# Softmax denominators in a two-layer DiT block: one 0/1 product and a wide reciprocal in place of a turn, a narrow reciprocal and a spread

## The chip, the cores and the metric

The kernel runs on one core of a Trainium2 chip. The metric is device microseconds for one execution. Engines are named as in the profile: PE is TensorE (PEld its weight loads), DVE is VectorE, ACT is ScalarE, POOL is GpSimd, SP is SyncE, whose queue issues the DMA transfers. All engines run their own instruction streams in order and wait for each other through semaphores.

## The reference, cut to what matters

The reference is a block of depth two over 512 tokens (and 256 context tokens) of width 1024, float32 throughout. Layer 0 is a Fourier/Hyena mixer, layer 1 is multi-head latent attention with 16 heads; a gated convolutional feed-forward part follows each. The change lies in the attention of layer 1:

```python
s = jnp.einsum('bqhd,bkhd->bhqk', qblk, k, preferred_element_type=jnp.float32) * scale
p = jax.nn.softmax(s, axis=-1).astype(v.dtype)
return jnp.einsum('bhqk,bkhv->bqhv', p, v)
```

For each of 16 heads there are 512 queries and 512 + 256 = 768 keys, 96 features for a score and 64 for a value. The kernel doesn't normalize the probabilities: it multiplies the values with exp(s - max) and divides the product, 64 rows by 512 queries, by the sum of the exponentials of each query. Only how these sums are brought together, inverted and brought to the rows of the product is changed.

## The kernel before, in words

Tokens lie along the free dimension and features on partitions. A float32 product that needs full precision is made of three single-pass products of high and low parts (`mm3`, lines 123 to 125) where both operands are split; other products are plain float32 (the profile shows two records, one weight load and one product each, per plain float32 product).

`attention` (line 949) first makes the latents, the values `V` and the normalized query latents. Then it goes over eight pairs of heads, p = 0 to 7. Three helpers make a pair:

- `qk(p)` (1081 to 1132): query and key projections of the pair (products into tiles `s` and `k2`), squares of them on ACT, their sums through small products into `ms` (lines 1100, 1112, 1114), a reciprocal square root on DVE (lines 1116 to 1120 and 132 to 141, some fourteen tiny instructions in a row), key parts `Kh` and `Kl` (ACT and DVE), and eight products with the identity that spread the roots over the tile (line 1130), with which DVE scales the queries (line 1131).
- `scores(p, a)` (1134 to 1156) for head a of the pair: six score tiles of 128 keys by 512 queries (three products each), copied to SBUF by ACT with the key's scale (line 1145) into two tiles `S` of three; maxima on DVE (lines 1146 to 1149), over the partitions on POOL (line 1151), and then, for each of the two tiles, the subtraction on DVE (line 1154, 128 x 1536) and the exponential on ACT (line 1155).
- `attend(p)` (1158 to 1186): 12 products with ones (line 1164), each 32 columns wide, which leave four partial sums of the denominators in four quarters of the PSUM tile `z`, two quarters a head; then the chain that is changed; 12 products with the values (line 1176), each 64 columns wide, two of which run side by side, into `pv`; and the product of `pv` with the row of inverted denominators into `O[p]` (line 1186).

The chain that is changed, before: ACT copies `z` to `zc` (1167). Four products turn it, 128 queries at a time, with a 128 x 2 matrix of zeros and ones as the moving operand, so that queries lie on partitions and the two columns are the sums of the two heads (1170). DVE inverts these 128 x 8 numbers (1172). Eight products with the identity spread them back over 64 partitions a head (1182). ACT copies that to `zrow` (1185), and line 1186 uses it. Each of `z`, `zt`, `zb` in the code is one tile of the same single PSUM buffer `z`, as `pv` is a single buffer, so the first product into each waits for the last reader of the one before.

The driving loop (lines 1188 to 1198) prepares two pairs ahead: in iteration p it emits `scores(p)`, `qk(p + 2)` and `attend(p - 1)`. The order in which the instructions stand on each engine is not this order but is made by the tile framework's scheduler when the kernel is built, with its own estimates; at run time every engine keeps to it. In what it made, PE has, ahead of the scores of pair p + 1, the eight spreading products of line 1130 of `qk(p + 2)`, which wait for the reciprocal square root on DVE. `attend(p - 1)` and `attend(p)` both fall into the same iteration for p = 1, 3 and 5, and none of them is finished in the iterations between, so that the iterations alternate in length. In this text iteration p runs from the first score product of pair p to the first of pair p + 1; those of p = 1, 3 and 5 are called long and those of p = 2 and 4 short. After the last pair the outputs `O` are split into high and low parts (`oh`, `ol`, lines 1209 and 1210), and the output projection `w_o` and the second feed-forward part follow.

Of the kernel before, what the change touches and what calls it, by code (L numbers as in the profile page):

```python
# [9 lines left out]
F32 = mybir.dt.float32  # L10
# [8 lines left out]
P = 128  # L19
# [31 lines left out]
class Builder:  # L51
# [897 lines left out]
    def attention(self, x, hh, hl, rest):  # L949
        nc, I = self.nc, self.I  # L950
        v = nc.vector
# [15 lines left out]
        ssp = self.t(pa, [P, 20], F32, "ssp")  # L967
        ones1 = self.ones32[:, 0:1]
        msk = self.t(pa, [P, 266], F32, "msk")
        rot, zsel, qm, ksel, s4 = msk[0:64, 0:128], msk[:, 128:130], msk[:, 256:258], msk[:, 258:260], msk[:, 260:264]  # L970
        qm32 = self.t(pa, [P, 2, 32], F32, "qm32")

        pt = self.pool("pt", bufs=2)
# [101 lines left out]
        pq = self.pool("pq", bufs=2)  # L1075
# [82 lines left out]
        def attend(p, Ss):  # L1158
            pv = self.t(psB, [P, 512], F32, "pv", 1)
            Z = lambda: self.t(psB, [P, 512], F32, "z", 1)  # L1160
            z = Z()
            for k in range(3):
                for g in range(4):
                    nc.tensor.matmul(z[32 * g : 32 * g + 32, :], self.ones32, Ss[g // 2][(2 * k + g % 2) // 3][:, (2 * k + g % 2) % 3, :], start=k == 0, stop=k == 2,  # L1164
                                     tile_position=(0, 32 * g))
            zc = self.t(pq, [P, 512], F32, "zc", 1)
            nc.scalar.copy(zc, z)
            zt = Z()
            for t_ in range(4):
                nc.tensor.matmul(zt[:, 2 * t_ : 2 * t_ + 2], zc[:, P * t_ : P * t_ + P], zsel, start=True, stop=True)  # L1170
            rz = self.t(pq, [P, 8], F32, "rz", 2)
            v.reciprocal(rz, zt[:, 0:8])
            for k in range(6):
                for a in range(2):
                    h = 2 * p + a
                    nc.tensor.matmul(pv[64 * a : 64 * a + 64, :], V[:, k, 64 * h : 64 * h + 64], Ss[a][k // 3][:, k % 3, :], start=k == 0, stop=k == 5,  # L1176
                                     tile_position=(0, 64 * a))
            zb = Z()
            for t_ in range(4):
                for a in range(2):  # L1180
                    g = 2 * t_ + a
                    nc.tensor.matmul(zb[64 * a : 64 * a + 64, P * t_ : P * t_ + P], rz[:, g : g + 1].to_broadcast([P, 64]), self.ident,
                                     start=True, stop=True, tile_position=(0, 64 * a))
            row = self.t(pq, [P, 512], F32, "zrow", 1)
            nc.scalar.copy(row, zb)
            v.tensor_tensor(O[p], pv, row, op=ALU.mult)

        prep = {0: qk(0), 1: qk(1)}
# [1 line left out]
        for p in range(KD):  # L1190
            qs, rs = prep.pop(p)
            Ss = [scores(p, a, qs[a], rs) for a in range(2)]
            if p + 2 < KD:
                prep[p + 2] = qk(p + 2)
            if prev:
                attend(*prev)
            prev = (p, Ss)
        attend(*prev)
        self.dbg("O", O)
        self.close("Sp")  # L1200
# [55 lines left out]
def constants():  # L1256
# [70 lines left out]
    am = np.zeros((P, 266))  # L1327
    j = np.arange(128)
    am[:64, 0:128] = (np.arange(64)[:, None] % 32) == (j[None, :] % 32)
    am[0::32, 128:130] = (np.arange(4)[:, None] // 2) == np.arange(2)[None, :]  # L1330
    am[:, 256] = np.arange(P) < 96
    am[:, 257] = (np.arange(P) < 32) | (np.arange(P) >= 64)
    am[:64, 258] = 1.0
# [86 lines left out]
def arrays_of(inputs):  # L1420
    a = layouts(**{k: np.asarray(v) for k, v in inputs.items()})
    a.update(constants())
    return {k: np.ascontiguousarray(v) for k, v in a.items()}
# [16 lines left out]
```

## Time and profile before

| What | us |
|---|---|
| Median of 3 runs (lowest, highest) | 1831.08 (1829.17, 1833.47) |
| Profiled execution | 1830.64 |
| Its span in the trace | 1828.8 |
| PE busy in the span | 1706.3 |
| DVE busy | 1022.0 |
| ACT busy | 613.9 |

In the profile "L1176" is line 1176 of the kernel before. A row of a group has the line, the engine, the operation, the tiles (out<-in), the shapes, the number of instructions, the total and the mean time, and the idle time of the engine ahead of them with what ended it. A row of the timeline has the start and the duration in us. A plain float32 product counts two matmul records. The two products of line 1170 and line 1182 write tiles that the profile names `z`, as the sums of line 1164 do.

### The profile page before, as it was taken

To read this page: it belongs to the slowest core of one execution; us is meant where nothing else is said; L and a number is where in the kernel's file an instruction comes from. 1 tells how busy PE (TensorE), PEld (TensorE's weight loads), DVE (VectorE), ACT (ScalarE), POOL (GpSimd) and SP (SyncE) were. 2 spreads that over 40 slices of the span, in tenths; PEclk is the share of its full clock that TensorE was granted. 3 is DMA by queue.
4 is the path that set the end of the run, shared out by engine and by line. 5 is a ranking of instruction groups with operands and counts; after the bars stand their busy time and mean duration, and the time that the engine had idled before them with its cause. 6 is when DMAs were issued, how large, how long until landed. Compare 5 with 4: busy or idle time off the path is not lost.

```text
span 1828.8 us, 21719 instructions
## 1 busy us (share of the span) xinstructions
PE 1706.3 (93%) x8742; PEld 1326.3 (73%) x8742; DVE 1022.0 (56%) x1662; ACT 613.9 (34%) x830; POOL 121.3 (7%) x202
## 2 busy tenths in 40 slices
PE   6889975799899999999999887899998999999999
PEld 2657864787688888888888556555554777888887
DVE  3486966864898435543434554665764554444443
ACT  3332222323323212222122434655663443223231
POOL 0052113310000000000000000110110000000000
PEclk7799987899999999999999998899999999999999
DMA  9032520352355234431312310000002323322322
GB/s 351 24 127 71 171 78 30 103 173 81 116 174 176 88 104 140 147 128 70 121 47 85 117 60 24 1 12 12 12 12 70 116 72 101 104 93 92 104 75 98
DMA packets 53249, 172.83 MB, mean 95 GB/s; under 512 B 6043, under 2 KB 8925, under 8 KB 52125
## 3 DMA queue, kind: packets, MB, share of 16 engines
q1 hardware_dynamic: 53149, 171.45, 27.4%
q8 instruction: 69, 1.13, 0.2%
q14 instruction: 31, 0.25, 0.0%
HBM read 167.23 MB, written 4.19 MB: 94 GB/s over the span
## 4 chain that ended last, share of the span: by engine, by line
PE 77%; DVE 11%; ACT 5%; POOL 3%; issue 3%; DMA 1%; POOLq 0%; SPq 0%; ACTq 0%; DVEq 0%
PE mm L123 21%; PE mm L124 20%; PE mm L125 20%; PE pv L1176 2%; PE ms L234 2%; PE z L1164 2%; DVE junk L210 2%; DVE wl L103 1%; DVE S L1154 1%; PE s L1130 1%; ACT S L1145 1%; PE s L123 1%; PE s L124 1%; PE s L125 1%; POOL s L388 1%
## 5 line engine op out<-in xcount | busy, mean ns | idle before, releaser
L123 PE MATMUL mm<-hh,wh 128*128 128x512 f32 (+2 forms) x1344 | 474.7, 356 | 7.0 <-ACT wh L98 3.4
L124 PE MATMUL mm<-hl,wh 128*128 128x512 f32 (+2 forms) x1344 | 473.9, 353 | 4.9 <-DVE hl L271 4.6
L125 PE MATMUL mm<-hh,wl 128*128 128x512 f32 (+2 forms) x1344 | 473.2, 353 | 1.3 <-DVE wl L103 1.3
L98 ACT ACTIVATE wh<-wr 128x1024 fp32r<-128x1024 f32 (+2 forms) x200 | 206.2, 1031 | 717.5 <-PE mm L124 646.5
L103 DVE TENSOR_TENSOR wl<-wr,wh 128x1024 fp32r<-128x1024 f32 (+2 forms) x200 | 243.6, 1219 | 287.3 <-ACT wh L98 279.6
L123 PEld LDWEIGHTS mm<-hh,wh 128*128 128x128 f32 x1344 | 254.4, 190 | 57.1 <-issue 12.0
L124 PEld LDWEIGHTS mm<-hl,wh 128*128 128x128 f32 x1344 | 255.0, 190 | 42.9 <-DVE hl L271 7.5
L125 PEld LDWEIGHTS mm<-hh,wl 128*128 128x128 f32 x1344 | 254.5, 190 | 38.4 <-issue 2.5
L123 PE MATMUL mm<-ah,wh 128*128 128x512 f32 (+1 forms) x528 | 187.8, 356 | 0.0
L124 PE MATMUL mm<-al,wh 128*128 128x512 f32 (+1 forms) x528 | 187.7, 356 | 0.0
L125 PE MATMUL mm<-ah,wl 128*128 128x512 f32 (+1 forms) x528 | 187.3, 355 | 0.0
L210 DVE SCALAR_TENSOR_TENSOR junk<-wr,sb 128x1024 bf16<-128x1024 f32 x128 | 159.3, 1244 | 36.7 <-DMA wr<-wmodT 36.6
L808 DVE SCALAR_TENSOR_TENSOR xr<-mm,mod,xr 128x512 f32<-128x512 f32 (+1 forms) x100 | 62.2, 642 | 204.3 <-PE mm L125 204.0
L123 PEld LDWEIGHTS mm<-ah,wh 128*128 128x128 f32 x528 | 99.1, 188 | 19.2 <-DVE xr L808 2.5
L124 PEld LDWEIGHTS mm<-al,wh 128*128 128x128 f32 x528 | 99.2, 188 | 15.3 <-issue 0.8
L125 PEld LDWEIGHTS mm<-ah,wl 128*128 128x128 f32 x528 | 99.2, 188 | 14.6
L1145 ACT ACTIVATE S<-s,rks 128x512 f32<-128x512 f32 x96 | 63.4, 688 | 44.3 <-PE s L125 43.4
L1154 DVE TENSOR_TENSOR S<-S,mb 128x1536 f32<-128x1536 f32 x32 | 54.8, 1752 | 20.7 <-POOL mb L1151 20.7
L845 ACT ACTIVATE fg<-fg 128x772 f32<-128x772 f32 (+1 forms) x44 | 32.6, 741 | 100.3 <-DVE fg L324 89.3
L1176 PE MATMUL pv<-S,V 128*64 128x512 f32 x192 | 58.9, 620 | 0.0
L1164 PE MATMUL z<-S,ones 128*32 128x512 f32 x192 | 42.7, 699 | 13.7 <-ACT S L1155 11.3
L1155 ACT ACTIVATE S<-S 128x1536 f32<-128x1536 f32 x32 | 47.1, 1481 | 18.0 <-DVE S L1154 18.0
(318 smaller groups left out, 2282.6 us busy)
## 6 DMA issues: line engine op xcount, KB each, us to landing
wr<-w_up SPq DMA_DIRECT2D x88, 512.0 KB, 3.3
wr<-wmodT SPq DMA_DIRECT2D x80, 512.0 KB, 3.3
wr<-w_dn SPq DMA_DIRECT2D x32, 512.0 KB, 3.2
wm<-wmod0a SPq DMA_DIRECT2D x8, 1024.0 KB, 9.6
wr<-w_in SPq DMA_DIRECT2D x16, 512.0 KB, 3.2
wr<-w_dn SPq DMA_DIRECT2D x20, 384.0 KB, 3.1
wr<-w_out SPq DMA_DIRECT2D x12, 512.0 KB, 3.2
wr<-w_o SPq DMA_DIRECT2D x12, 512.0 KB, 3.2
```

The costliest lines, as they stand in the source:

```text
L98: self.nc.scalar.activation(dst, src, AF.Copy)
L103: (eng or self.nc.vector).tensor_tensor(dst, src, hi.bitcast(F32), op=ALU.subtract)
L123: mmul(out, wh, xh, start=start, stop=False)
L124: mmul(out, wh, xl, start=False, stop=False)
L125: mmul(out, wl, xh, start=False, stop=stop)
L210: nc.vector.scalar_tensor_tensor(junk, raw, 1.0, self.sb[:, j, :], op0=ALU.mult, op1=ALU.mult, accum_out=acc)
L808: nc.vector.scalar_tensor_tensor(x[m][:, a2:b2], ps[:, a2:b2], mod[:, 8 * sec + m, j : j + 1], x[m][:, a2:b2], op0=ALU.mult, op1=ALU.add)
L1145: nc.scalar.activation(S[j // 3][:, j % 3, :], ps, AF.Copy, scale=rs[:, 2 * j + a : 2 * j + a + 1])
L1154: v.tensor_tensor(s, s, mb3.to_broadcast([P, 3, T]), op=ALU.subtract)
L1155: nc.scalar.activation(s, s, AF.Exp)
L1164: nc.tensor.matmul(z[32 * g : 32 * g + 32, :], self.ones32, Ss[g // 2][(2 * k + g % 2) // 3][:, (2 * k + g % 2) % 3, :], start=k == 0, sto ...
L1176: nc.tensor.matmul(pv[64 * a : 64 * a + 64, :], V[:, k, 64 * h : 64 * h + 64], Ss[a][k // 3][:, k % 3, :], start=k == 0, stop=k == 5, tile ...
```

## The change

The turning products, the narrow reciprocal, the spreading products and ACT's copy go. In their place, one product has a 128 x 128 matrix of zeros and ones (`zsum`) as the stationary operand and `zc` as the moving one: each of its 128 output rows is the sum of the two quarters of its head, so the denominators of all 512 queries stand on all 64 rows of each head at once. DVE then takes the reciprocal of the whole 128 x 512 tile out of PSUM into `zrow`. `msk` keeps its size; the matrix takes columns that were empty.

```diff
-        rot, zsel, qm, ksel, s4 = msk[0:64, 0:128], msk[:, 128:130], msk[:, 256:258], ...
+        rot, zsum, qm, ksel, s4 = msk[0:64, 0:128], msk[:, 128:256], msk[:, 256:258], ...
...
             zt = Z()
-            for t_ in range(4):
-                nc.tensor.matmul(zt[:, 2 * t_ : 2 * t_ + 2], zc[:, P * t_ : P * t_ + P], zsel, start=True, stop=True)
-            rz = self.t(pq, [P, 8], F32, "rz", 2)
-            v.reciprocal(rz, zt[:, 0:8])
+            nc.tensor.matmul(zt, zsum, zc, start=True, stop=True)
+            row = self.t(pq, [P, 512], F32, "zrow", 1)
+            v.reciprocal(row, zt)
             for k in range(6):
...
-            zb = Z()
-            for t_ in range(4):
-                for a in range(2):
-                    g = 2 * t_ + a
-                    nc.tensor.matmul(zb[64 * a : 64 * a + 64, P * t_ : P * t_ + P], rz[:, g : g + 1].to_broadcast([P, 64]), self.ident,
-                                     start=True, stop=True, tile_position=(0, 64 * a))
-            row = self.t(pq, [P, 512], F32, "zrow", 1)
-            nc.scalar.copy(row, zb)
             v.tensor_tensor(O[p], pv, row, op=ALU.mult)
...
-    am[0::32, 128:130] = (np.arange(4)[:, None] // 2) == np.arange(2)[None, :]
+    am[0::32, 128:256] = (np.arange(4)[:, None] // 2) == (j[None, :] // 64)
```

The scheduler makes a new order from the changed program. What it moves on PE and DVE, in iteration p = 3 (lines in the numbering of the kernel before; products are counted, not records):

```
DVE before: ... subtract x2 | reciprocal 128x8 | ql | max 1146 | qt | max 1147, 1148, 1149 | wl | subtract x2 | qt |
            nrm_s | Kl | 1117 | O2 | 132 | Kl | 133 | reciprocal 128x8 | 9 tiny | 1120 | 1131 x2
DVE after:  ... subtract x2 | reciprocal 128x512 | max 1146 | qt | max 1147, 1148 | qt | max 1149 | O2 | subtract x2 |
            nrm_s | Kl | 1117 | ql | 132 | wl | 133 | Kl | 4 tiny | reciprocal 128x512 | 2 tiny | O3 | 3 tiny | 1120 | 1131 x2
PE before:  ... 10 of line 1164 | 1 of 1176 | 4 of 1170 | 2 of 1176 | 6 of k2 | 2 of 1176 | line 1130 | scores
PE after:   ... 1 of 1176 | 5 of 1164 | 2 of 1176 | 5 of 1164 | 2 of 1176 | 1 of 1170 | 6 of k2 | 7 of 1176 | line 1130 | scores
```

In p = 5 the order is of the same kind, without the six k2 products and with O5 ahead of the seven tiny instructions; in p = 1 the ten sums of line 1164 stay together, ten products of line 1176 stand ahead of line 1130, and no O stands between the second reciprocal and the tiny instructions. In both kernels the last pairs have their own order; there the changed kernel has the reciprocal of pair 6 and O6 between the maxima 1146 and 1149 of the last head.

More of the change, by code (lines that the diff above doesn't have):

```diff
@@ L969, in attention @@
         msk = self.t(pa, [P, 266], F32, "msk")
-        rot, zsel, qm, ksel, s4 = msk[0:64, 0:128], msk[:, 128:130], msk[:, 256:258], msk[:, 258:260], msk[:, 260:264]
+        rot, zsum, qm, ksel, s4 = msk[0:64, 0:128], msk[:, 128:256], msk[:, 256:258], msk[:, 258:260], msk[:, 260:264]
         qm32 = self.t(pa, [P, 2, 32], F32, "qm32")
```

## The prediction

> **What bounds the kernel now.** I read the page first, then the timeline and the stretches around the attention of layer 1.
>
> ```profile
> span 1828.8 us, 21719 instructions
> ...
> PE 1706.3 (93%) x8742; PEld 1326.3 (73%) x8742; DVE 1022.0 (56%) x1662; ACT 613.9 (34%) x830; POOL 121.3 (7%) x202
> ...
> PE 77%; DVE 11%; ACT 5%; POOL 3%; issue 3%; DMA 1%; POOLq 0%; SPq 0%; ACTq 0%; DVEq 0%
> ```
>
> PE is busy and carries most of the chain, DVE comes second. All that changes lies between 1130 and 1400 us. By stretches (limits, length, busy time with counts of PE, PEld, DVE, ACT, POOL, then the granted clock):
>
> ```profile
> 1130.00:1400.00 270.00, 248.92 (x1249) 141.91 (x1250) 171.20 (x271) 155.67 (x206) 28.55 (x16) 0.94 0.05 18
> ...
> 1236.00:1297.00 61.00, 60.21 (x319) 35.55 (x317) 37.98 (x62) 35.90 (x50) 7.13 (x4) 0.99 0.03 10
> ...
> 1301.00:1305.00 4.00, 3.83 (x17) 1.78 (x14) 3.63 (x16) 1.83 (x2) 0.00 (x0) 0.57 0.00 0
> ```
>
> No engine is full there: DVE works 171 of 270 us. What counts is order and waiting. The first score products of pairs 1 to 6 (PE timeline) cut it into iterations:
>
> ```profile
> 1171.34 0.48 PE L123 MATMUL s<-qh,Kh 128*128 128x512 f32 x1
> ...
> 1207.95 0.47 PE L123 MATMUL s<-qh,Kh 128*128 128x512 f32 x1
> ...
> 1239.35 0.48 PE L123 MATMUL s<-qh,Kh 128*128 128x512 f32 x1
> ...
> 1275.77 0.48 PE L123 MATMUL s<-qh,Kh 128*128 128x512 f32 x1
> ...
> 1307.01 0.48 PE L123 MATMUL s<-qh,Kh 128*128 128x512 f32 x1
> ...
> 1342.89 0.47 PE L123 MATMUL s<-qh,Kh 128*128 128x512 f32 x1
> ```
>
> Long ones take 36.6, 36.4 and 35.9 us, short ones 31.4 and 31.2. Both divisions fall into the long ones. The long iteration of pair 3, by the timeline:
>
> ```profile
> 1249.65 3.43 DVE L1154 TENSOR_TENSOR S<-S,mb 128x1536 f32<-128x1536 f32 x2 [1.98 <-POOL mb L1151]
> ...
> 1251.77 2.79 PE L1176 MATMUL pv<-S,V 128*64 128x512 f32 x12
> ...
> 1255.57 1.23 DVE L1146 TENSOR_TENSOR mx<-S,S 128x1024 f32<-128x1024 f32 x1 [1.82 <-ACT S L1145]
> ...
> 1257.44 0.68 DVE L1147 TENSOR_TENSOR mx<-mx,S 128x512 f32<-128x512 f32 x1
> 1258.04 0.68 DVE L1148 TENSOR_TENSOR mx<-mx,S 128x512 f32<-128x512 f32 x1
> 1258.76 0.69 DVE L1149 TENSOR_TENSOR mx<-mx 128x512 f32<-128x512 f32 x1
> ...
> 1260.36 1.04 PE L1182 MATMUL z<-cst,rz 128*64 128x128 f32 x12
> ...
> 1261.67 3.42 DVE L1154 TENSOR_TENSOR S<-S,mb 128x1536 f32<-128x1536 f32 x2
> ...
> 1263.67 2.93 ACT L1155 ACTIVATE S<-S 128x1536 f32<-128x1536 f32 x2
> ...
> 1265.99 2.77 PE L1164 MATMUL z<-S,ones 128*32 128x512 f32 x20
> ...
> 1269.70 1.05 PE L1170 MATMUL z<-msk,zc 128*128 128x2 f32 x8
> ...
> 1270.79 0.21 DVE L1172 RECIPROCAL rz<-z 128x8 f32<-128x8 f32 x1 [1.60 <-PE z L1170]
> ...
> 1272.57 0.18 DVE L141 SCALAR_TENSOR_TENSOR rq_r<-rq_b,rq_r 128x20 f32<-128x20 f32 x1
> ...
> 1273.96 2.05 PE L1130 MATMUL s<-cst,rq_r 128*128 128x128 f32 x16
> ```
>
> The reader is to see one rope: subtraction for head 0, maxima, POOL, subtraction and exponential for head 1, its sums, the small reciprocal, the nine tiny root instructions queued behind it on DVE, line 1130, the next scores. PE's own work just covers it at the end: the root is ready at 1272.75, PE gets to line 1130 at 1273.96.
>
> **The change part by part.** Prices, from groups by shape (from the stretch 1130 to 1400, and of the whole run for line 412, which has the very shape, PSUM source included, of the added reciprocal) and one row of the timeline for the nearest full-width float32 product:
>
> ```profile
> L1182 PE MATMUL z<-cst,rz 128*64 128x128 f32 x128 | 13.8, 278 | 0.0
> ...
> L1170 PE MATMUL z<-msk,zc 128*128 128x2 f32 x64 | 8.4, 254 | 0.0
> ...
> L1185 ACT COPY zrow<-z 128x512 f32<-128x512 f32 x8 | 4.7, 584 | 15.5 <-PE z L1182 15.5
> ...
> L1172 DVE RECIPROCAL rz<-z 128x8 f32<-128x8 f32 x8 | 1.6, 205 | 14.3 <-PE z L1170 14.3
> ...
> L412 DVE RECIPROCAL S<-ms 128x512 f32<-128x512 f32 x2 | 6.7, 3346 | 0.0
> ...
> 103.48 1.13 PE L410 MATMUL ms<-s,on 128*128 128x512 f32 x2 [0.70 <-POOL s L394]
> ```
>
> - Turn (1170): 1.05 us a pair goes, a full product comes. Line 410 bounds it by 1.13 from above; four side-by-side value products of two records (2.79 for 12 records, six products in three turns) give 0.93 from below. I take 0.95: nothing gained or lost.
> - Spread (1182): 13.8 us of summed durations, but pieces overlap; twelve of a pair's sixteen records take 1.04 in the long iteration and the other four run beside the last value product: some 1.2. Between 0 and 13.8 / 8 = 1.7. Off PE it frees at most 8 x 1.2 = 9.8 us, where PE is the end of the rope.
> - Copy (1185): 0.58 us less of ACT a pair, seldom at the end of anything.
> - Reciprocal: 3.35 - 0.21 = 3.14 us more of DVE a pair, 25.1 in all. DVE has the room (171 + 25 of 270), but not at these places.
> - SP and POOL keep their instructions; transfers (5% share here) are not what is late.
>
> [...]
>
> Long iteration, pair 3, followed in the changed order. Head 0's subtraction ends at 1253.08. The first wide reciprocal comes next, to 1256.43 (its product is done long before). The maximum 1146 had waited for ACT till 1255.57, so only 0.86 is lost here; with one more `qt` ahead of 1149 (0.6, as from 1147 to 1148, from start to start) 1149 ends at about 1260.75 instead of 1259.45. POOL takes the usual 1.98, head 1's subtraction starts at 1262.7 instead of 1261.67, its exponentials end at 1267.75 (+1.15). PE has no spread to do and waits for them. The sums are now cut: five after the first exponential (from 1266.1; ten took 2.77 in three turns of up to four, five take two turns, 1.85), two value products (1.0), five sums (1.85), two value products (1.0): 1271.8, the new product to 1272.7, where the turn ended at 1270.75. The second reciprocal runs to 1276.1. Behind it on DVE stands O3, which needs all value products. PE does k2 first (from the turn's start to line 1130 passed 4.26, less 1.05 and two turns of value products leaves 1.3), then seven value products in four turns of 0.93: 1277.7. O3 0.6, three tiny ones (nine took 1270.95 to 1272.75, 0.2 each) and line 1130 starts at 1279.05: **+5.1**. Pair 5: no k2, seven tiny instructions after O5: 1272.7 + 3.72 + 0.6 + 1.5 = 1278.6, **+5.2** against its own start. Pair 1: sums uncut, the product ends at 1271.5, ten value products in five turns and k2 end at 1277.4, and the root is ready by 1276.4: **+3.3**. Together +13.6. From below: with the product where the turn ended, the reciprocal and 1.5 us of tiny work still make line 1130 start at 1275.7, +1.7 each, 5 in all.
>
> Short iterations (pair 4), by DVE's timeline and PE's:
>
> ```profile
> 1292.96 0.68 DVE L1149 TENSOR_TENSOR mx<-mx 128x512 f32<-128x512 f32 x1
> ...
> 1295.88 0.18 DVE L1116 TENSOR_TENSOR nrm_s<-ms,ssp 128x20 f32<-128x20 f32 x1 [2.24 <-PE ms L1114]
> ...
> 1296.85 3.41 DVE L1154 TENSOR_TENSOR S<-S,mb 128x1536 f32<-128x1536 f32 x2
> ...
> 1305.20 2.05 PE L1130 MATMUL s<-cst,rq_r 128*128 128x128 f32 x16
> ```
>
> Here something is won. DVE waited 2.24 for key sums that stood behind value products and the spread on PE; those are gone, so the subtraction follows POOL at 1293.64 + 1.98 = 1295.62: 1.2 earlier. In pair 4, O (0.6) leaves the stretch too: -1.9. In pair 2 it stays, and PE's sums and k2 products after the exponentials hold the gain to some -0.9. From above: 0 each.
>
> The end, where nothing else covers:
>
> ```profile
> 1381.06 3.43 DVE L1154 TENSOR_TENSOR S<-S,mb 128x1536 f32<-128x1536 f32 x2 [1.35 <-POOL mb L1151]
> ...
> 1384.45 3.62 PE L1164 MATMUL z<-S,ones 128*32 128x512 f32 x10 [3.36 <-ACT S L1155]
> ...
> 1392.93 1.05 PE L1170 MATMUL z<-msk,zc 128*128 128x2 f32 x8
> ...
> 1399.15 0.69 DVE L1186 TENSOR_TENSOR O<-pv,zrow 128x512 f32<-128x512 f32 x1 [4.91 <-ACT zrow L1185]
> ```
>
> The reciprocal of pair 6 and O6 stand among the last head's maxima (+3.14 and +0.6, less 0.6 for O5 and about 1 of a wait for ACT): +2.0 on the last subtraction. Then product at 1394.9 to 1395.9, reciprocal to 1399.25, the last value products to 1399.6; O7 at 1399.65 instead of 1399.15, since spread and copy are gone: **+0.5** net.
>
> Sum: 13.6 - 0.9 - 1.9 + 0.5 = +11.3 on 1830.64, its own execution: 1841.9. That execution lies 0.44 under the median of the runs shown, so I say 1842.
>
> **The rivals.** First, DVE's slack hides every reciprocal and PE's saving counts. It needs the rope to end on PE: that PE, not the root, is what line 1130 waits for, by more than the 3.14 that DVE gains. The stretch shows 1.2 us of such room (1272.75 to 1273.96), and PE's 98.7% busy between the scores of pair 3 and the first wait speaks for it. Then the 9.8 of above go: 1821. It decides the sign if the second reciprocal starts before about 1269, before its sums are done in the old order.
>
> Second, every reciprocal lies on the rope in full and no short iteration gives back: 8 x 3.14 = 25, less the spread and copy at the very end (1.8): 1854. Against it: head 0's reciprocal falls partly into DVE's 1.82 us of waiting for ACT.
>
> Third, the clock. The stretch 1301 to 1305 shows 0.57 of the granted clock after PE had waited; such a stretch costs 4 x 0.43 = 1.7 us. Long iterations show none now. If the longer waits put one into each, 3 x 1.7 = 5.2 come on top: 1847. [...]
>
> Fourth, gains and losses cancel, as with +1.7 for each long iteration, 3.1 won in the short ones and 1.8, the spread and the copy, at the end, the last head's maxima being covered: 1831. For it speaks that the floor is a floor, against it that head 1's exponentials are late by more than a microsecond in each long iteration.
>
> **How the numbers follow.** Chances: forecast 0.65, its own range from 1833 (floors of the long iterations and all gains of the short ones) to 1848 (5.2 in each long iteration, no gain in the short ones, 2.0 at the end). Clock 0.08, full price 0.05, cancelling 0.07, hidden 0.15. What a measurement of this kernel can tell from no change is about 0.2%, 3.7 us. Slower is forecast, clock and full price: 0.78; same 0.07; faster 0.15. The range leaves out hidden and full price, 0.20: from 1831 to 1850.
>
> **What would show it.** Long iterations of 40 to 41.5 us and short ones of 29 to 30.5 in the starts of the scores; eight reciprocals of 3.35 us on DVE; ahead of line 1130, PE waiting for DVE where it did not; the tiny root instructions behind O and the reciprocal; after pair 6 a later last subtraction but an O7 at about the same distance. I am wrong if long iterations don't grow (the product comes much earlier than I place it), if the sums of line 1164 start without waiting for head 1's exponentials, or if the weight of the order is not where I put it, in the root that waits behind O3 and O5.

## The result, and the profile after

The changed kernel takes 1847.03 us in the median (1845.24 to 1847.29), the kernel before 1831.08 (1829.17 to 1833.47): 1.0084 times as long, 95% interval 1.0069 to 1.0098. The prediction was 1842, range 1831 to 1850. The profiled execution of the changed kernel has a time of 1847.03 and a span of 1845.3, 16.5 more than the 1828.8 of before. The page of the changed kernel:

```profile
span 1845.3 us, 21359 instructions
PE 1705.7 (92%) x8566; PEld 1319.4 (72%) x8566; DVE 1045.3 (57%) x1662; ACT 609.8 (33%) x822; POOL 121.5 (7%) x202
PE 75%; DVE 13%; ACT 5%; POOL 4%; issue 3%; DMA 0%; POOLq 0%; SPq 0%; DVEq 0%; ACTq 0%
```

PE has 176 product records fewer and yet the same busy time; DVE and POOL have won shares of the chain, PE has lost some. Cut by the first score products of pairs 1 to 6 and the start of the last output product O7, the stretches of the changed kernel are these (limits, length, busy time with counts of PE, PEld, DVE, ACT, POOL, then the granted clock):

```profile
1170.50:1211.38 40.88, 38.97 (x181) 19.93 (x180) 28.96 (x39) 20.58 (x27) 3.56 (x2) 0.92 0.04 14
1211.38:1241.77 30.39, 24.25 (x117) 15.43 (x116) 21.50 (x36) 18.22 (x24) 3.57 (x2) 0.83 0.00 1
1241.77:1285.79 44.02, 41.60 (x180) 18.85 (x178) 29.54 (x40) 20.44 (x27) 3.56 (x2) 0.92 0.04 12
1285.79:1316.44 30.65, 23.56 (x106) 15.71 (x105) 20.98 (x35) 18.23 (x24) 3.56 (x2) 0.80 0.00 1
1316.44:1357.82 41.38, 38.17 (x182) 18.68 (x181) 30.60 (x40) 21.52 (x28) 3.56 (x2) 0.98 0.08 26
1357.82:1414.31 56.49, 45.99 (x176) 19.34 (x175) 35.13 (x32) 32.58 (x43) 7.13 (x4) 0.94 0.11 37
```

The same view of the kernel before, for the three long iterations:

```profile
1171.34:1207.95 36.61, 36.49 (x198) 20.96 (x196) 23.16 (x39) 21.02 (x28) 3.56 (x2) 1.00 0.04 15
...
1239.35:1275.77 36.42, 36.30 (x194) 20.09 (x192) 23.16 (x39) 20.92 (x28) 3.56 (x2) 1.00 0.04 15
...
1307.01:1342.89 35.88, 35.76 (x192) 19.49 (x190) 23.15 (x39) 20.92 (x28) 3.56 (x2) 1.00 0.08 30
```

Long iterations carry 5.8 to 7.5 us more of DVE (two reciprocals) and are 4.3, 7.6 and 5.5 us longer. The granted clock, full in all three before, is now 0.92, 0.92 and 0.98. The table sets this beside the forecast and the experiments told below; the lengths are differences of the starts in the profiled execution of each kernel, the ratio is that of all runs to the kernel before on the same chip.

| Kernel | pair 1 | 2 | 3 | 4 | 5 | 6 to O7 | sum | ratio (95%) |
|---|---|---|---|---|---|---|---|---|
| before | 36.61 | 31.40 | 36.42 | 31.24 | 35.88 | 56.26 | 227.81 | 1 |
| forecast | 39.9 | 30.5 | 41.5 | 29.3 | 41.1 | 56.8 | 239.1 | 1.006 |
| changed | 40.88 | 30.39 | 44.02 | 30.65 | 41.38 | 56.49 | 243.81 | 1.0084 (1.0069 to 1.0098) |
| copy on DVE | 36.52 | 31.76 | 37.80 | 32.73 | 36.47 | 54.56 | 229.84 | 1.0019 (1.0010 to 1.0028) |
| copy on ACT | 36.38 | 31.34 | 37.66 | 30.97 | 36.19 | 53.43 | 225.97 | 1.0003 (0.9991 to 1.0015) |
| before + wide reciprocal | 40.30 | 30.66 | 41.71 | 30.31 | 40.94 | 58.67 | 242.59 | 1.0085 (1.0073 to 1.0097) |
| changed + spread products | 39.26 | 29.61 | 42.28 | 30.64 | 41.86 | 56.55 | 240.20 | 1.0068 (1.0054 to 1.0082) |
| odd pairs behind the root | 37.44 | 33.58 | 40.19 | 31.67 | 38.26 | 56.97 | 238.11 | 1.0059 (1.0046 to 1.0072) |
| even pairs behind the maximum | 39.93 | 30.84 | 37.51 | 34.64 | 43.41 | 54.92 | 241.25 | 1.0082 (1.0065 to 1.0099) |
| both orders | 37.37 | 33.12 | 37.61 | 34.61 | 40.83 | 55.50 | 239.04 | 1.0059 (1.0046 to 1.0071) |
| sums in SBUF, later orders | 37.78 | 33.40 | 37.78 | 33.65 | 36.71 | 56.99 | 236.31 | 1.0053 (1.0041 to 1.0066) |

So 16.0 of the 16.5 us of span lie between the scores of pair 1 and O7. The long iteration of pair 3 in the changed kernel, by the timeline:

```profile
1255.43 3.35 DVE L1171 RECIPROCAL zrow<-z 128x512 f32<-128x512 f32 x1
...
1262.54 0.69 DVE L1096 TENSOR_TENSOR qt<-s,tab 128x512 f32<-128x512 f32 x1 [0.88 <-ACT sq L1094]
...
1264.49 0.61 PE L1112 MATMUL ms<-msk,cp 128*128 128x4 f32 x4 [0.47 <-ACT cp L1107]
...
1265.82 3.43 DVE L1154 TENSOR_TENSOR S<-S,mb 128x1536 f32<-128x1536 f32 x2 [1.38 <-POOL mb L1151]
...
1269.15 3.62 PE L1164 MATMUL z<-S,ones 128*32 128x512 f32 x10 [0.54 <-ACT S L1155]
...
1274.07 1.90 PE L1164 MATMUL z<-S,ones 128*32 128x512 f32 x10
...
1276.91 1.13 PE L1169 MATMUL z<-zc,msk 128*128 128x512 f32 x2
...
1278.08 3.36 DVE L1171 RECIPROCAL zrow<-z 128x512 f32<-128x512 f32 x1 [4.06 <-PE z L1169]
...
1279.04 3.65 PE L1175 MATMUL pv<-S,V 128*64 128x512 f32 x14
...
1282.72 0.69 DVE L1177 TENSOR_TENSOR O<-pv,zrow 128x512 f32<-128x512 f32 x1 [1.05 <-PE pv L1175]
...
1283.98 2.05 PE L1130 MATMUL s<-cst,rq_r 128*128 128x128 f32 x16 [1.30 <-DVE rq_r L141]
```

The rope of the prediction is there: reciprocal, head 1's subtraction, its sums, product, second reciprocal, O3, the rest of the root, and line 1130, which now waits 1.30 us for DVE. Two things stand out. Five of the sums (ten records, x10) take 3.62 us at 1269.15 and the other five 1.90 at 1274.07; and the second reciprocal has waited 4.06 us on DVE, with half of the root behind it. The first is the clock, by the stretches around, and by a finer cut of where it falls:

```profile
1262.00:1266.50 4.50, 3.92 (x28) 2.11 (x25) 2.58 (x4) 2.29 (x5) 1.78 (x1) 1.00 0.00 0
1266.50:1274.00 7.50, 6.96 (x18) 1.26 (x18) 7.33 (x14) 3.78 (x3) 0.00 (x0) 0.54 0.11 29
1274.00:1284.00 10.00, 8.70 (x39) 3.00 (x37) 4.75 (x9) 0.58 (x1) 0.00 (x0) 1.00 0.08 30
...
1266.00:1267.00 1.00, 1.00 (x8) 0.91 (x8) 1.00 (x1) 0.00 (x0) 0.00 (x0) 0.82 0.00 0
1267.00:1268.00 1.00, 1.00 (x2) 0.00 (x0) 1.00 (x2) 0.39 (x1) 0.00 (x0) 0.50 0.00 0
```

Over these 7.5 us the granted clock is 0.54. It is at 0.50 from 1267 on, and PE's wait of 0.54 us for head 1's exponentials begins only at 1268.61, so the fall comes ahead of that wait. In pair 1 it is the same: the granted clock is 0.50 from 1195.00 on, and the wait of 1.33 us for the exponentials, which ends at 1196.92, begins 0.6 us later, at 1195.59:

```profile
1195.00:1196.90 1.90, 0.58 (x4) 0.49 (x3) 1.90 (x2) 1.48 (x1) 0.00 (x0) 0.50 0.04 9
```

In the waits from 1130 to 1420 us (waiting line, releaser: total, times, longest) the pair of names grows to

```profile
PE z L1164 <- ACT S L1155: 25.0, 12, 5.1
```

from this, in the kernel before, from 1130 to 1400:

```profile
PE z L1164 <- ACT S L1155: 11.3, 6, 3.4
```

Little of this growth lies in the long iterations: there these waits are 1.3, 0.5 and 0.6 us, where the kernel before has none. Most of it lies in pairs 2 and 4 (5.5 and 6.5 us instead of 1.7 and 2.0) and behind pair 6's scores (7.1 instead of 4.2).

### The profile page after: what moved, and what is told of

Its sections match the earlier page's. It is cut to its first block, busy times and chain, and to the rows that moved or that the text cites. A ratio compares the mean times of both kernels' runs of the same rounds, so it can differ in the third digit from the quotient of the medians.

```text
span 1845.3 us, 21359 instructions
## 1 busy us (share of the span) xinstructions
PE 1705.7 (92%) x8566; PEld 1319.4 (72%) x8566; DVE 1045.3 (57%) x1662; ACT 609.8 (33%) x822; POOL 121.5 (7%) x202
## 4 chain that ended last, share of the span: by engine, by line
PE 75%; DVE 13%; ACT 5%; POOL 4%; issue 3%; DMA 0%; POOLq 0%; SPq 0%; DVEq 0%; ACTq 0%
PE mm L123 22%; PE mm L124 21%; PE mm L125 21%; PE ms L234 2%; DVE S L1154 2%; PE pv L1175 2%; POOL mb L1151 1%; PE z L1164 1%; ACT S L1145 1%; PE s L1130 1%; DVE junk L210 1%; DVE wl L103 1%; POOL s L388 1%; ACT wh L98 1%; DVE nt L266 1%
## 5 line engine op out<-in xcount | busy, mean ns | idle before, releaser
L1145 ACT ACTIVATE S<-s,rks 128x512 f32<-128x512 f32 x96 | 62.8, 687 | 57.6 <-PE s L125 56.8
L1164 PE MATMUL z<-S,ones 128*32 128x512 f32 x192 | 47.2, 765 | 27.8 <-ACT S L1155 25.0
```

Source lines behind the costliest of these rows:

```text
L1145: nc.scalar.activation(S[j // 3][:, j % 3, :], ps, AF.Copy, scale=rs[:, 2 * j + a : 2 * j + a + 1])
```

## The experiments

Two theories stood against each other, and a third beside them. Theory Q: the loss is the length of the reciprocal in DVE's queue, which runs in order and stands in the chain from one pair's scores to the next. Rival P: the spread products dropped from PE are worth time that the reciprocal then eats. Rival C: a part of the loss is PE's lower clock after longer waits. None of the edits changes a length alone: for each the scheduler makes a new order. With a copy in the reciprocal's place, for example, O2 stands behind head 1's subtraction in pair 3's iteration, where the changed kernel has it ahead. So what is due to the length and what to the order that it brings about isn't separated by removing or adding the reciprocal.

**The reciprocal replaced by a copy on DVE.** The products are dropped, but no long instruction comes.

```diff
-            v.reciprocal(row, zt)
+            v.tensor_copy(row, zt)
```

> The changed kernel with DVE's wide reciprocal replaced by a plain DVE copy of the same 128 x 512 tile; the inversion is left out, so the outputs are not normalized. Theory Q (the length of the reciprocal on DVE's in-order queue makes the loss): the loss of 16 us goes and some of PE's saving of at most 9.8 us shows, 1821 to 1831 us. Rival P (PE's own new order, with the sums cut in two and the values early, makes the loss): it stays at 1840 or more. Rival C (the lower clock after PE's waits is half of the loss by itself, whatever caused the waits): 1835 to 1840, with stretches at half the clock still in the long iterations.

Measured: 1832.00 us against 1827.92 of before on the same chip, ratio 1.0019 (1.0010 to 1.0028). Without the reciprocal's length three quarters of the loss are gone, but nothing is won over the kernel before, though the spread is gone too. With the kernel before at 1831 the ratio gives 1834.5. Rival P's 1840 or more is excluded; Q's 1821 to 1831 is missed by 3.5 us, and C's 1835 to 1840 begins just above. The granted clock of the long iterations is 1.00, 0.91 and 0.95, so low stretches are left in pairs 3 and 5.

**The reciprocal alone, in the kernel before.** All else of the change is left undone.

```diff
             rz = self.t(pq, [P, 8], F32, "rz", 2)
+            wide = self.t(pq, [P, 512], F32, "wide", 1)
+            v.reciprocal(wide, zc)
```

> The kernel before, with one more instruction a pair: DVE takes the reciprocal of the whole 128 x 512 tile zc into a tile that nobody reads. Turn, narrow reciprocal, spread and ACT's copy stay. Theory Q: DVE's time alone is enough, so at least the changed kernel's 1847, and up to 1857 since PE keeps its spread. Rival P: PE's products are those of before, 1831 to 1836.

Measured: 1843.75, ratio 1.0085 (1.0073 to 1.0097), the loss of the whole change. Its long iterations:

```profile
1167.88:1208.18 40.30, 39.91 (x217) 22.55 (x216) 29.06 (x41) 20.98 (x28) 3.57 (x2) 1.00 0.04 14
...
1238.84:1280.55 41.71, 40.30 (x214) 21.57 (x212) 29.07 (x41) 20.87 (x28) 3.57 (x2) 1.00 0.04 13
...
1310.86:1351.80 40.94, 39.53 (x218) 21.32 (x216) 29.54 (x42) 21.45 (x29) 3.57 (x2) 1.00 0.08 27
```

They are 3.7, 5.3 and 5.1 us longer than before, at a full clock: the +3.3, +5.1 and +5.2 of the prediction, without the clock's share. That the whole loss is as large even so comes in good part from the end, 58.67 us from pair 6's scores to O7 instead of 56.26. Nothing reads the wide tile, so I take it to act through its 3.35 us a pair in DVE's queue and the order that the scheduler makes with it. Rival P's 1831 to 1836 are excluded; Q's "at least the changed kernel's" is just met.

**The copy on ACT.** The copy on DVE is itself 0.69 us a pair; on ACT it leaves DVE with less work than before. The inversion is left out here as in the first run.

```diff
-            v.reciprocal(row, zt)
+            nc.scalar.copy(row, zt)
```

> Changed kernel with ScalarE's copy in the place of VectorE's reciprocal; the inversion is left out, so the time is that of a kernel without it. The earlier run with VectorE's copy stood 4 us above the kernel before, with less work on TensorE and 0.69 us of copy in the place of 0.21 us of reciprocal on VectorE. Theory Q: these 4 us are the copy's length on VectorE, and with VectorE freed of it the time is that of the kernel before or up to 4 us less (1827 to 1831 with the kernel before at 1831). Rival P (the dropped spread products are worth TensorE's time once VectorE does not stand in the way): 6 to 10 us under the kernel before, 1821 to 1825. Rival C (the dropped products had kept TensorE busy in its waits, and without them the clock is lower): 2 to 5 us above the kernel before still, with a granted clock of the span under 0.956.

Measured: 1830.46 against 1830.57, ratio 1.0003 (0.9991 to 1.0015). Its long iterations:

```profile
1169.38:1205.76 36.38, 35.64 (x174) 18.67 (x172) 22.82 (x37) 21.54 (x29) 3.56 (x2) 1.00 0.04 15
...
1237.10:1274.76 37.66, 36.76 (x170) 18.04 (x168) 22.81 (x37) 21.53 (x29) 3.56 (x2) 0.95 0.04 14
...
1305.73:1341.92 36.19, 35.28 (x167) 17.09 (x166) 22.82 (x37) 21.53 (x29) 3.56 (x2) 1.00 0.09 30
```

PE runs some 24 records fewer than before in each and is still busy for 97 to 98% of the time (35.64 of 36.38), and these iterations are 0.2 shorter, 1.2 and 0.3 longer than before. Only behind pair 6's scores is something won, 2.8 us. Rival P's 6 to 10 us fall, and so do rival C's 2 to 5 us more: the span's clock is 0.958 in the profiled execution, as in that of before. Even with no inversion at all the changed kernel only reaches the kernel before, and none of the orders of the wide reciprocal tried below comes under this run.

**The spread products put back, unread.** DVE's order of instructions is that of the changed kernel; PE gets eight products a pair that nobody needs.

```diff
+            zb = Z()
+            for t_ in range(4):
+                for a in range(2):
+                    g = 2 * t_ + a
+                    nc.tensor.matmul(zb[64 * a : 64 * a + 64, P * t_ : P * t_ + P], row[:, g : g + 1].to_broadcast([P, 64]), self.ident,
+                                     start=True, stop=True, tile_position=(0, 64 * a))
             v.tensor_tensor(O[p], pv, row, op=ALU.mult)
```

> Changed kernel with the eight spread products of each pair put back on TensorE, reading columns of the reciprocal and read by nothing; VectorE's order of instructions is that of the changed kernel, so only work on TensorE is added, some 1.2 us for each pair. Theory C2 (dropping the products bought no time, because the long iterations wait for VectorE's chain, and cost some, because TensorE pauses there longer and is clocked lower after it): the granted clock of the iterations of pairs 1 and 3 rises from 0.92 to 1.00, pair 1's falls from 40.9 to about 40.3 us and pair 3's from 44.0 to about 41.7, as in the run of the kernel before with an unread wide reciprocal, and the time is 1 to 4 us less than the changed kernel's: 1843 to 1846 with the kernel before at 1831. Rival P (TensorE's work is on the path and dropping it had paid part of the reciprocal): 5 to 10 us more than the changed kernel, 1852 to 1857.

Measured: 1843.43, ratio 1.0068 (1.0054 to 1.0082); rival P's 5 to 10 us more are excluded. Whether it is faster than the changed kernel the intervals don't settle (1.0069 to 1.0098 there); the profiled executions show a gain at the places named. Long iterations 1 and 3:

```profile
1168.04:1207.30 39.26, 38.03 (x198) 20.52 (x196) 28.95 (x39) 20.52 (x27) 3.57 (x2) 1.00 0.05 14
...
1236.91:1279.19 42.28, 41.80 (x212) 21.07 (x210) 29.54 (x40) 20.48 (x27) 3.56 (x2) 1.00 0.04 13
```

and their sums, with pair 3's second reciprocal, by the timeline:

```profile
1194.42 3.57 PE L1164 MATMUL z<-S,ones 128*32 128x512 f32 x20 [0.59 <-ACT S L1155]
...
1264.63 1.90 PE L1164 MATMUL z<-S,ones 128*32 128x512 f32 x10
...
1271.48 3.36 DVE L1171 RECIPROCAL zrow<-z 128x512 f32<-128x512 f32 x1 [2.32 <-PE z L1169]
```

The clock is 1.00 in both. The first five sums behind head 1's exponentials in pair 3 (x10) take 1.90 where the changed kernel took 3.62, the reciprocal waits 2.32 instead of 4.06, and the iteration is 1.74 shorter. In pair 1 the ten sums (x20) take 3.57 instead of

```profile
1196.92 5.17 PE L1164 MATMUL z<-S,ones 128*32 128x512 f32 x20 [1.33 <-ACT S L1155]
```

in the changed kernel, and the iteration is 1.62 shorter. These are single executions, but the clock over the span bears them out: 0.953 to 0.958 in the five executions of this kernel, 0.950 or 0.951 in those of the changed one. So these two iterations lost 1.6 and 1.7 us to the clock; pair 2 gained 0.8, pair 5 lost 0.5.

**The reciprocal twice.** A dose: the first result goes to a tile that nobody reads.

```diff
+            junk = self.t(pq, [P, 512], F32, "zjunk", 1)
+            v.reciprocal(junk, zt)
             v.reciprocal(row, zt)
```

> The reciprocal of the 128x512 denominators is computed twice for each pair on VectorE, the first time into a tile that nothing reads. Theory Q (the loss is the reciprocal's length in VectorE's queue, which stands in the chain from one pair's scores to the next pair's): the second 3.35 us costs about what the first did; taking the copy instead of the reciprocal away gave back 15 us, so another 12 to 18 us, and about 1.7% over the kernel before (1859 to 1865 if that stands at 1831). Rival H (the first reciprocal only used up a gap, and further ones pile up beside other work): under 6 us more, 1848 to 1853. Rival C (the loss is mainly the lower granted clock after TensorE's longer waits): more than the dose, 20 us or more, with the granted clock of the span under 0.945.

Measured: 1869.38, ratio 1.0213 (1.0195 to 1.0231), 24 us (1.29%) over the changed kernel. Rival H's under 6 is excluded. The total is beyond Q's 12 to 18, and what rival C had named (20 or more at a clock under 0.945): the profiled execution, the slowest of the five, has a granted clock of 0.943, the median one 0.945. But the second group is 26.7 us long, so nearly its full length on the chain would give the same; this run doesn't tell the two apart:

```profile
L1172 DVE RECIPROCAL zjunk<-z 128x512 f32<-128x512 f32 x8 | 26.8, 3354 | 9.6 <-PE z L1169 9.6
...
L1173 DVE RECIPROCAL zrow<-z 128x512 f32<-128x512 f32 x8 | 26.7, 3342 | 0.0
```

The profiled execution is 26.3 us longer in its span than that of the changed kernel. Of these, 17.6 lie between pair 1's scores and O7, within Q's 12 to 18; the rest wasn't traced to a cause, and 6.5 of it lie ahead of pair 0's scores, where the two kernels are alike. The first reciprocal costs 15 us by the ratios (1.0084 against 1.0003 with ACT's copy), and 17.8 between pair 1's scores and O7 by the table. So by the totals the second costs more than the first, but in the stretch that holds all eight of either they cost the same, some two thirds of their length. That the second found less room isn't shown.

**The order on DVE.** Ordering edges put reciprocal and O of pairs 1, 3 and 5 behind the root instructions.

```diff
-            v.reciprocal(row, zt)
+            behind = rooted.get(p + 2) if p % 2 else None    # instruction of line 1120
+            with self.tc.issue_after(behind.ins) if behind else ExitStack():
+                v.reciprocal(row, zt)
...
+            with self.tc.issue_after(behind.ins) if behind else ExitStack():
+                v.tensor_tensor(O[p], pv, row, op=ALU.mult)
```

> The changed kernel with one ordering edge for pairs 1, 3, 5: their reciprocal and their last product O stand on DVE behind the root instructions of the pair that is being prepared. Theory Q: PE's waits for the root ahead of line 1130 (1.30, 0.54 and 2.15 us in the changed kernel's trace) go, 1843 to 1844 us. Rival P and rival C: 1846 to 1848, since the waits for head 1's exponentials stay.

Measured: 1839.77, ratio 1.0059 (1.0046 to 1.0072), so 1842 with the kernel before at 1831. The long iterations are 3.4, 3.8 and 3.1 shorter than in the changed kernel, pairs 2 and 4 are 3.2 and 1.0 longer, with more of PE's records in them:

```profile
1207.66:1241.24 33.58, 30.14 (x133) 16.41 (x132) 21.46 (x36) 18.23 (x24) 3.56 (x2) 0.90 0.00 0
...
1281.43:1313.10 31.67, 25.77 (x126) 15.56 (x124) 22.78 (x37) 19.28 (x25) 3.56 (x2) 0.84 0.00 1
```

The changed kernel has 117 and 106 there. Theory Q's number, 3 to 4 us won, is met and somewhat passed, and the 1846 to 1848 of P and C are excluded, though part of what the long iterations gave went to the short ones.

**The other reciprocal moved.** Reciprocals of pairs 0, 2 and 4 behind head 1's last maximum of the next pair.

```diff
+            behind = maxed.get((p + 1, 1)) if p % 2 == 0 else None    # last maximum, line 1149
```

> Changed kernel, with the reciprocal and the output product of pairs 0, 2 and 4 ordered behind the last maximum of head 1 of the next pair; the other pairs as the scheduler likes. This takes these reciprocals out of the long iterations (pairs 1, 3, 5) at the place where they stand ahead of a maximum and of a subtraction, and leaves the ones that stand ahead of the root. Theory Q: in the long iterations 3.35 us less stand in the chain where the reciprocal of the earlier pair is the one on the path; the edge for the other pairs gave back 7 us of 19, so this one gives 4 to 10 us (1837 to 1843 if the kernel before stands at 1831). Rival S (VectorE's total load in a long iteration decides, wherever the reciprocal stands in it): within 2 us of the changed kernel, 1845 to 1849.

Measured: 1843.60, ratio 1.0082 (1.0065 to 1.0099): with the kernel before at 1831 that is 1846, so Q's number is missed and rival S's holds. What happened shows in pairs 3 and 4:

```profile
1239.38:1276.89 37.51, 31.61 (x139) 16.81 (x138) 25.93 (x38) 19.85 (x26) 3.56 (x2) 0.86 0.05 14
1276.89:1311.53 34.64, 34.62 (x166) 17.63 (x164) 25.38 (x38) 20.69 (x27) 3.56 (x2) 1.00 0.00 1
```

One reciprocal left pair 3 (DVE 25.93 instead of 29.54) and came with its attention's products into pair 4 (PE x166 instead of x106). Pair 3 won 6.5 us, pair 4 lost 4.0, pair 5 lost 2.0. With both edges together:

```diff
+            behind = rooted.get(p + 2) if p % 2 else maxed.get((p + 1, 1))
```

> Changed kernel with both ordering edges of the earlier runs: reciprocal and output product of pairs 1, 3 and 5 behind the root instructions of the pair prepared, those of the even pairs behind head 1's last maximum of the next pair. Theory Q: each edge takes another reciprocal off the chain, and what they gave singly (7 and 3 us) adds up, so 1836 to 1839 with the kernel before at 1831. Rival S (the reciprocals, off one place of the chain, land at another): no better than the better of the two, 1839 to 1843.

Measured: 1840.73, ratio 1.0059 (1.0046 to 1.0071), no better than the first edge alone. The edges don't add up; rival S again.

**The sums out of PSUM, and later edges.** ACT copies the sums to SBUF, which frees the PSUM buffer for the next pair's sums, and both reciprocals are put where I took DVE to have room: the even pairs' behind head 1's last subtraction of the next pair, the odd pairs' behind the root.

```diff
+            zsb = self.t(pq, [P, 512], F32, "zsb", 1)
+            nc.scalar.copy(zsb, zt)
+            behind = rooted.get(p + 2) if p % 2 else lowered.get((p + 1, 1))    # root, or head 1's subtraction
...
-                v.reciprocal(row, zt)
+                v.reciprocal(row, zsb)
```

> The changed kernel with both reciprocals off the chain: ACT copies the sums to SBUF (so the PSUM tile comes free), and ordering edges put the reciprocal of pairs 0, 2, 4, 6 behind head 1's subtraction of the next pair and that of pairs 1, 3, 5 behind the root instructions. Theory Q: head 1's exponentials are on time again and nothing waits for the reciprocal: 1822 to 1832 us. Rival P: 1842 to 1848.

Measured: 1838.87, ratio 1.0053 (1.0041 to 1.0066), or 1841 with the kernel before at 1831. Q's 1822 to 1832 is missed, and it is also just under P's 1842. The long iterations come to 37.78, 37.78 and 36.71, near those of before, but the short ones grew to 33.40 and 33.65. In pair 2 DVE waits for the key sums of line 1115, and PE has 14 records of the earlier pair's value products ahead of them:

```profile
1231.13 0.18 DVE L1117 TENSOR_TENSOR nrm_s<-ms,ssp 128x20 f32<-128x20 f32 x1 [2.78 <-PE ms L1115]
```

The later a reciprocal runs, the later its attention lets go of `pv`, which O reads, and of `z`, which the reciprocal itself reads unless the sums are copied out as here; the next attention's products move with it. With the even pairs behind the maximum (line 1165 there is line 1164 of the changed kernel), PE's waits for the reciprocal to be done with `z` grow to this from 2.8 us in the changed kernel:

```profile
PE z L1165 <- DVE zrow L1174: 8.4, 2, 4.9
```

**Two tries to keep PE busy in its waits**, both failed as tests of the clock, since they moved the order. First, three unread products for each of pairs 0 to 5 (the expectation names too few), ahead of the sums:

```diff
+            if p + 2 < KD:
+                with self.tc.issue_after(keyed[p + 2].ins):    # last product of line 1114
+                    for _ in range(3):
+                        nc.tensor.matmul(z[64:128, :], V[:, 0, 0:64], Ss[0][0][:, 0, :], start=True, stop=True, tile_position=(0, 64))
```

> Changed kernel, with three unread products of 512 columns for each attention of pairs 0 to 3, which write rows of the bank that are rewritten later and stand behind the last key-norm product of the pair prepared, so that TensorE has something to do where it waits for the exponentials. Rival C (the lower granted clock after these waits makes what the loss exceeds the forecast by, some 5 us): half-clock stretches after the waits go, the span's clock rises to 0.955 or more, and the time falls by 2 to 6 us to 1841 to 1845 (with the kernel before at 1831). Theory Q alone: TensorE's products are not what is waited for, and the three more only add themselves or nothing: 1846 to 1850.

Measured: 1860.35, ratio 1.0162 (1.0147 to 1.0178), beyond both. In pair 0's iteration, which grew from 29.6 to 35.1 us, all sums came to stand behind these products, which took long themselves:

```profile
1164.85 5.02 PE L1166 MATMUL z<-S,V 128*64 128x512 f32 x6
```

Second, three unread products on the result of POOL, in the changed kernel and in the kernel before alike:

```diff
+            if a == 1:
+                hot = S1()
+                for _ in range(3):
+                    nc.tensor.matmul(hot, self.ident, mb, start=True, stop=True)
```

> Changed kernel with three unread products of 512 columns behind head 1's maximum over the partitions in every pair. They change the scheduler's order: each pair's iteration then holds one attention, where the changed kernel has two in every other iteration and parts of none in the rest. Theory Q: in an even order the reciprocal of each pair still stands in VectorE's queue within the chain, so the time is above that of the kernel before with the same three products by 8 to 20 us. Rival B (the loss comes from the uneven order, where two reciprocals fall into one iteration): in the even order the difference is under 5 us.

> Kernel before with the same three unread products behind head 1's maximum over the partitions. It is what the run of the changed kernel with these products is to be compared with. The three products are some 3 us of TensorE for each pair, and TensorE has 2 to 3 us of waits in every second iteration: 1831 to 1850, and under 1831 only if the even order of attentions saves more than the products cost.

Measured: 1904.06 (ratio 1.0411, 1.0396 to 1.0425) and 1898.64 (1.0375, 1.0361 to 1.0390), both far above what was expected (1831 to 1850 for the kernel before). PE's queue stops at these products until POOL is done, as in this row of the changed kernel with them:

```profile
1250.11 2.84 PE L1156 MATMUL s<-mb,cst 128*128 128x512 f32 x6 [1.89 <-POOL mb L1151]
```

The difference between the two is 5.4 us by the medians and 6.6 by the ratios. With intervals of some 3 us to either side of each ratio that lies between Q's 8 to 20 and rival B's under 5 and decides for neither. In this even order, with one attention in each iteration of 43 to 46 us, the change costs 5.4 to 6.6 us instead of the 16 of the other. So its price seems to depend on the order that it falls into.

## Why the prediction was right, and where it was off

- *Turn to one product, nothing gained or lost.* The new product's row is 1.13 us, line 410's, not the 0.95 that I took; 0.08 more than the turn.
- *Reciprocal, 3.35 us.* The price was the 3346 ns of line 412's row; eight of them in the group of the changed kernel, 3355 ns each:

```profile
L1171 DVE RECIPROCAL zrow<-z 128x512 f32<-128x512 f32 x8 | 26.8, 3355 | 17.7 <-PE z L1169 17.7
```

- *Spread, between nothing and 9.8 us of PE* (8 x 1.2 is 9.6; it changes nothing). It was nothing that the times can tell: the run with ACT's copy stands at 1.0003. The first rival, hidden, had a chance of 0.15, and PE's 98.7% of busy time spoke for it. It was no ground: without these products the share is about the same and the long iterations are at most 0.2 us shorter.
- *Long iterations +3.3, +5.1, +5.2.* Measured +4.3, +7.6, +5.5. The mechanism was the one followed through pair 3, and the run with the wide reciprocal in the kernel before gives +3.7, +5.3, +5.1. In the changed kernel the sums of pairs 1 and 3 came on top, 5.17 - 3.57 = 1.6 and 3.62 - 1.90 = 1.7, at a granted clock of 0.53 and 0.50 where the run with the spread products put back shows 1.00. The rest of pair 3's excess lies earlier: the second `qt` ahead of its maximum 1149 waits 0.88 for ACT, for which the forecast had no term, so that head 1's subtraction comes at 24.05 into the iteration instead of 23.35.
- *Short iterations -0.9 and -1.9.* Measured -1.0 and -0.6. Pair 4's gain was mis-sized, again by the clock: its line 1130 takes 3.78 us, at a granted clock of 0.50, where it took 2.05 at 1.00.

```profile
1308.96 1.93 PE L1164 MATMUL z<-S,ones 128*32 128x512 f32 x6 [5.07 <-ACT S L1155]
1313.01 3.78 PE L1130 MATMUL s<-cst,rq_r 128*128 128x128 f32 x16 [0.54 <-DVE rq_r L141]
```

- *The end, +0.5.* Measured +0.2.
- *The third rival, the clock, +5.2 over the sum.* It was no other way of going but a term of the forecast: 1.6 + 1.7 + 1.7 = 5.0, in pairs 1, 3 and 4 instead of 1, 3 and 5. With it, 11.3 becomes 16.3, where the iterations show 16.0. That it was set apart, with a chance of 0.08, is the step that failed: the forecast priced everything behind head 1's exponentials at a full clock. The rival's own ground, a low stretch after PE's longer waits, isn't shown either, since in pairs 1 and 3 the clock falls before PE waits for the exponentials. And that 16.3 and 16.0 lie so close is in part luck: with its share of the clock, pair 1 came out 0.6 under its forecast, pair 3 0.8 over and pair 4 0.4 under.
- *Full price, 25 us, and cancelling, 0.* Neither came.
- *The signs.* Pair 3's 44.0 us lies above the 40 to 41.5 that were named and pair 4's 30.65 above the 29 to 30.5; the other iterations lie within. PE waits for the root ahead of line 1130 in pairs 3 and 5 (1.3 and 2.1 us), where it did not before, and O7 comes at 56.49 from pair 6's scores instead of 56.26.

## What to carry to other kernels

Price a longer instruction where it stands in its engine's queue, iteration by iteration; the same change cost 2 us a pair in one order of the work and 0.7 to 0.8 in another. Work dropped from PE, which waits for the same chain, bought nothing here, however busy PE looked. The stretches of low clock moved with the order here: the sums of pairs 1 and 3 and pair 4's line 1130, at a granted clock of 0.50 to 0.53, cost some 5 of the 16 us, and with the spread products put back the sums ran at 1.00. A forecast should carry the clock as a term of the sum. When an order edge takes an instruction off one iteration, follow the buffers that it holds: the work behind them moves too.

## What the runs showed of the hardware that was not expected

Eight useless products a pair on TensorE did not cost time: the ratio is 1.0068 with them against 1.0084 without, with intervals that overlap, and between pair 1's scores and O7 the profiled executions take 240.20 against 243.81 us. The sums of pairs 1 and 3 keep the full clock.

The granted clock averaged 0.54 over 7.5 us where PE had hardly waited at all. From pair 3's first scores at 1241.77 to 1268 us, this is PE's only wait in the changed kernel:

```profile
PE ms L1112 <- ACT cp L1107: 0.5, 1, 0.5
```

What lies around it are products of 2 and 4 columns (lines 1112 and 1114), which the records show as busy. But these products don't lower the clock by themselves: the kernel before has them in its long iterations too, at a clock of 1.00. In the 4.50 us ahead of the stretch PE is busy for 3.92, so here a PE that the profile shows busy, with one wait of 0.5 us since its scores began, did not keep its clock. Nor do the gaps alone tell: with the spread products put back, PE is idle for 1.21 of these 4.40 us in pair 1, among the same small products, and keeps its clock:

```profile
1190.00:1194.40 4.40, 3.19 (x25) 2.09 (x24) 3.52 (x3) 3.18 (x4) 1.06 (x1) 1.00 0.00 0
```

What makes the clock fall, these runs don't show. The length of a low stretch, at a granted clock of 0.50, they do show: in windows of half a us it is 3.4 us in pair 4 of the kernel before, and in the changed kernel 6.8 in each of pairs 1 and 3, 10.2 in pair 2 and 13.7 from pair 4 into pair 5, so two, three and four times the 3.4.
